# Fewer weight blocks split ahead at the end of the down products, and three of a chunk's additions to x by ScalarE and a transfer

## The chip, the core and the metric

The kernel runs on one core of a Trainium2 chip. The metric is the device time of one execution in microseconds (us). The engines are TensorE (PE; its weight loads are PEld), VectorE (DVE), ScalarE (ACT), GpSimd (POOL) and SyncE (SP); all run beside each other and wait for each other by semaphores. Transfers are issued by SP, ACT or POOL and are carried out by 16 DMA engines.

## What is computed

A decoder trunk of two layers on x of 1024 tokens by 1024 channels in float32. Each layer adds a mixer, a cross attention on a memory of 256 tokens and a feed-forward part (hidden width 2816) to x, each on a normalised x:

```python
def rmsnorm(x, g):
    xf = x.astype(jnp.float32)
    y = xf * lax.rsqrt(jnp.mean(xf * xf, axis=-1, keepdims=True) + EPS)
    return (y * g.astype(jnp.float32)).astype(x.dtype)

def swiglu(h, w_gate_up, w_down):
    g, u = jnp.split(h @ w_gate_up, 2, axis=-1)
    return (jax.nn.silu(g) * u) @ w_down

def reference(...):
    for layer in range(DEPTH):
        h = rmsnorm(x, norm_mix_g[layer])
        ...
        x = x + mix
        mem_n = rmsnorm(mem, mem_norm_g[layer])
        x = x + memory_cross_attention(rmsnorm(x, norm_xattn_g[layer]), mem_n, ...)
        x = x + swiglu(rmsnorm(x, norm_ffn_g[layer]), ffn_w_gate_up[layer], ffn_w_down[layer])
    return rmsnorm(x, final_norm_g)
```

## The kernel before

x stands transposed in SBUF: 16 tiles of 128 channels by 512 tokens, `xT[h][k]` (h is the half of the tokens, k the block of channels). Each float32 product is made of three float32r matmuls (`mm3`): each operand is split into a high part (a cast by ScalarE, L344 for weights, tile whi) and a low part (a subtraction by VectorE, L345, tile wlo). There are four buffers for each part of a weight block.

Large products use a scheme of seven block products in place of eight: sums of weight blocks (s1 to s4) meet sums of operands (t1 to t4). The weight sums are made by transfers that accumulate in SBUF, which POOL issues (`add_to`, L339). Each sum has a due time, and `pair_blocks` gives the blocks of one pair out in a fixed order.

The feed-forward part (`ffn`) runs over 22 blocks of the hidden width. For each, `gate_up` makes gate and up products in seven weight blocks of 12 matmuls; their evacuations by ScalarE (L2038) and VectorE lead to a tile of hidden values. Two such tiles make a chunk: after the third, fifth and each further odd number of blocks, `down.out(c)` multiplies chunk c with its part of the down weights (class `Down`). `Down.FORM` lists the seven weight blocks of a chunk, the operand, the group of four PSUM banks (a, b or c) that it goes into, and the part of x. For each of a block's four pieces m, `out` issues three matmuls and one VectorE instruction that adds the bank to x or subtracts it (L204); a bank that is used again is accumulated further. There are eight PSUM banks in all. Ten chunks go this way in each of the two layers; the last two blocks go through `outproj` (`down_last`). The operands of a later chunk are built beside this by `build`, spread by `pace`, which only the feed-forward's `Down` has.

What is issued when is set by a planner that runs while the program is written: `Threads` holds generators by rank, and a clock `now` that each matmul moves on by 0.42 ns per column. `prefetch` splits weight blocks until `ahead` of them are ready (3 in most of `ffn`), but a sum only when by that clock it has landed, unless `block` needs it at once. `Step` holds a transfer back until it is due. The order in which the text issues instructions gives their rank; the program places one that is ready before one that is not.

`norm_stats` sums squares over the channels with matmuls (ssq), works out the inverse root (ncol) and, `D2` of planned time later, broadcasts it with matmuls (rbp) for the evacuations. `late_stats` calls it with a delay that comes from D1 or D3. The first mixer, both cross attentions and the second mixer use it; the feed-forward's norm (`norm_quarter`) doesn't.

Of the kernel before, what the change touches and what calls it, by code (L numbers as in the profile page):

```python
# [9 lines left out]
F32 = mybir.dt.float32  # L10
# [8 lines left out]
P = 128  # L19
# [3 lines left out]
HT = 512  # L23
# [9 lines left out]
class Event:  # L33
    def __init__(self):
        self.at = None
# [80 lines left out]
class Down:  # L116
# [10 lines left out]
    def __init__(self, t, tags, eng=None, sign=1, pace=None):  # L127

        self.t, self.tags, self.eng, self.sign, self.pace = t, list(tags), eng or t.nc.vector, sign, pace
        t.th.free[self] = len(self.tags)  # L130
        self.over = {-1: Event()}
        t.th.set(self.over[-1])
        self.full, self.right, self.ev = {}, {}, {}

# [18 lines left out]
    def build(self, c):  # L153
# [8 lines left out]
        def operand(nm, src, fresh=True):  # L162
            if self.pace and fresh:
                yield self.pace / 2
            yield (self, 2)
            self.right[c, nm] = self.parts(src, self.eng)
            t.th.set(self.ev[c][nm], 2500)
            if self.pace:
                yield self.pace / 2 if fresh else self.pace
# [16 lines left out]
        t.nc.vector.scalar_tensor_tensor(b11, b11, -1.0, b21, op0=ALU.mult, op1=ALU.subtract)  # L186
        yield from operand("t4", b11)

    def out(self, c):
        t, nc, banks = self.t, self.t.nc, {}  # L190
        for w, r, to, i, h, sign in self.FORM:
            hi, lo = t.block()
            t.prefetch()
            yield self.ev[c][r]
            op = "tensor_add" if sign * self.sign > 0 else "tensor_sub"
            rh, rl, mine = self.right.pop((c, r))
            for m in range(4):
                new = (to, m) not in banks
                if new:
                    banks[to, m] = t.ps("dn")  # L200
                ps = banks[to, m]
                t.mm3(ps, [(hi[:, m, :], lo[:, m, :])], [(rh, rl)], first=new, onto=not new)
                x = t.xT[h][4 * i + m]
                getattr(nc.vector, op)(x, x, ps)  # L204
                t.prefetch()
                if m % 2:
                    yield 0
            self.give(mine)
        t.th.set(self.over[c])


# [10 lines left out]
class Trunk:  # L222
# [4 lines left out]

    D1, D2, D3 = 15000, 6000, 20000  # L230
    PARTS = ((0, slice(0, HT)), (1, slice(0, 256)), (1, slice(256, HT)))
    BUFS = {"xg": 32, "g": 20, "o": 8, "p": 7, "pt": 4, "r": 4, "rb": 2}
    RAWS = 5
# [30 lines left out]
    def mm(self, out, lhsT, rhs, start=True, stop=True, onto=False):  # L264
        n = rhs.free_size() if hasattr(rhs, "free_size") else int(np.prod(rhs.shape[1:]))
        self.th.now += max(n * (0.42 if rhs.dtype != F32 else 1.69), 55.0)
        self.nc.tensor.matmul(out, lhsT, rhs, start=start, stop=stop, skip_group_check=onto)  # L267

    def tr(self, out, src, k=P):
        self.th.now += 109.0  # L270
        self.nc.tensor.transpose(out, src, self.ident[:k, :k])  # L271
# [228 lines left out]
    def late_stats(self, N, h, rows):  # L500

        nc, acc = self.nc, None
        yield 3000
        for t in self.xT[h]:
            sq = self.g("p" if acc else "pt", name="sq")
            nc.scalar.activation(sq, t, AF.Square)
            if acc is None:
                acc = sq
            else:
                nc.vector.tensor_add(acc, acc, sq)  # L510
            yield 800
        yield from self.norm_stats(N, h, acc, rows, (self.D1 if rows else self.D3) - 9400)

    def norm_half(self, N, h, gname, off=0, rows=True):

# [1498 lines left out]
    def ffn(self, N, layer, on_half, on_block=None):  # L2014
        nc, th = self.nc, self.th
        last = FB // 2 - 1
        hid, hid_ev = [[None, None], [None, None]], [Event(), Event()]
        down = Down(self, ["pt"] * 4 + ["g"] * 4 + ["r"] * self.BUFS["r"], nc.vector, -1, 2400)
# [83 lines left out]
        def gate_up_plain():  # L2102

            ws = [[], []]

            def evac(h, gp, up):
                yield N.rb_ev[h]
                t = self.g("p", name="f")
                nc.vector.tensor_mul(t, gp, N.rb[h])
                yield 1500  # L2110
                nc.scalar.activation(t, t, AF.Silu)
                yield 1200
                nc.vector.scalar_tensor_tensor(t, t, -1.0, up, op0=ALU.mult, op1=ALU.mult)
                nc.vector.tensor_mul(t, t, N.rb[h])
                yield from hidden(0, h, t)

            for h, first, second in ((0, "11", "21"), (1, "12", "22")):
                ps = [self.ps("gu"), self.ps("gu")]
                for i, b in enumerate((first, second)):
                    yield N.b_ev[b]  # L2120
                    for n in range(2):
                        if h == 0:
                            ws[i].append(self.block())
                        self.mm3(ps[n], self.ks(ws[i][n]), N.b[b], i == 0, i == 1)
                        if h == 0 and i == 0:
                            self.prefetch()
                        yield 0
                    if b == "12":
                        th.set(N.free12, 0)
                        self.prefetch()  # L2130
                th.spawn(evac(h, *ps))

        def down_last():
            return self.outproj(hid, hid_ev, on_half, on_block=on_block, sub=True)

        for j in range(FB):
            self.ahead = 3 if 0 < j < FB - 1 else 2
            yield from gate_up(j) if j else gate_up_plain()
            if j == 1:
                yield N.rb_ev  # L2140
            if j % 2 == 0 and j:
                yield from down.out(j // 2 - 1)
        yield from down_last()


# [109 lines left out]
```

## Time and profile before

| | us |
|---|---|
| median of three timed runs | 2538.11 |
| lowest and highest of them | 2534.14, 2538.69 |
| the profiled execution | 2531.58 |
| its span, first to last instruction | 2529.9 |
| TensorE busy in the span | 2473.7 |
| VectorE busy | 1955.1 |
| ScalarE busy | 1082.3 |
| GpSimd busy | 450.9 |

An engine's busy time is the union of its instructions' times. Matmuls are pipelined, so that one starts before the last has ended: a stretch in which TensorE is always busy can still be longer than its matmuls need. In the views below, "a <- b" after an idle time says which instruction ended the wait. Names such as wraw<-wraw are what an instruction writes and reads.

### The profile page before, as it was taken

What the parts mean: (1) busy time and instruction counts of PE and PEld (TensorE: products, weight loads), DVE (VectorE), ACT (ScalarE), POOL (GpSimd) and SP (SyncE); (2) the same over time, 40 slices, a digit from 0 to 9 for tenths busy, and PEclk for the clock granted to TensorE, in tenths of its full rate; (3) what the DMA queues carried; (4) which work ended last, traced back from release to release, by engine and by line L of the source; (5) the groups of instructions that cost most, each with busy time, mean ns of one, the idle gap of its engine ahead of it and who ended that gap; (6) DMA issues with size and microseconds to landing.
All of it is one profiled execution on the core that took longest, in us unless ns stands there. A gap on an engine that the chain in (4) does not pass through costs nothing.

```text
span 2529.9 us, 34429 instructions
## 1 busy us (share of the span) xinstructions
PE 2473.7 (98%) x12029; PEld 2027.8 (80%) x12029; DVE 1955.1 (77%) x3789; ACT 1082.3 (43%) x2125; POOL 450.9 (18%) x487
## 2 busy tenths in 40 slices
PE   9999999999999999999999999999999999999998
PEld 7788888777777777779998788788777777777777
DVE  5777779988888887774638788787998777888887
ACT  5322555533333333343324367575554333333333
POOL 5411021121222122110000120001111212121222
PEclk9999999999999999999999999999999999999999
DMA  5232212455555555511122132122135555555552
GB/s 139 54 83 81 92 47 58 87 120 121 118 122 117 115 125 122 116 42 39 39 50 55 31 81 72 46 84 51 45 80 122 118 115 117 117 122 120 119 119 97
DMA packets 300093, 227.33 MB, mean 90 GB/s; under 512 B 28911, under 2 KB 250320, under 8 KB 299920
## 3 DMA queue, kind: packets, MB, share of 16 engines
q1 hardware_dynamic: 226688, 150.28, 20.5%
q0 software_dynamic: 72912, 74.32, 18.9%
q8 instruction: 95, 1.56, 0.3%
q14 instruction: 78, 0.64, 0.1%
q10 hardware_dynamic: 320, 0.53, 0.1%
HBM read 176.84 MB, written 4.19 MB: 72 GB/s over the span
## 4 chain that ended last, share of the span: by engine, by line
PE 75%; DVE 13%; DMA 4%; issue 4%; ACT 3%; POOL 1%; SPq 0%; DVEq 0%; ACTq 0%; POOLq 0%
PE gu L267 25%; PE pj L267 14%; PE dn L267 12%; PE op L267 6%; DVE x L204 4%; PE tp L267 4%; DMA wraw<-wraw 3%; DVE wlo L345 3%; PE as L267 2%; PE ao L267 1%; DMA wraw<-in_ffn_w_down_dram 1%; DVE fh L139 1%; PE apt L271 1%; PE o L267 1%; PE kps L267 1%
## 5 line engine op out<-in xcount | busy, mean ns | idle before, releaser
L344 ACT CAST whi<-wraw 128x512 fp32r<-128x512 f32 (+1 forms) x652 | 398.8, 617 | 929.4 <-DMA wraw<-wraw 207.7
L345 DVE TENSOR_TENSOR wlo<-wraw,whi 128x512 fp32r<-128x512 f32 (+1 forms) x652 | 442.2, 686 | 176.4 <-ACT whi L344 170.4
L267 PE MATMUL dn<-fh,whi 128*128 128x512 f32 x1456 | 459.9, 397 | 14.7 <-DVE x L204 11.0
L204 DVE TENSOR_TENSOR x<-x,dn 128x512 f32<-128x512 f32 x728 | 451.5, 677 | 0.3 <-PE dn L267 0.2
L267 PEld LDWEIGHTS dn<-fh,whi 128*128 128x128 f32 x1456 | 266.1, 188 | 100.8 <-issue 22.8
L267 PE MATMUL dn<-fh,wlo 128*128 128x512 f32 x728 | 286.0, 393 | 0.0
L267 PE MATMUL gu<-xth,whi 128*128 128x512 f32 x672 | 267.2, 398 | 8.9 <-DVE f L2063 3.1
L267 PE MATMUL gu<-xtl,whi 128*128 128x512 f32 x672 | 264.9, 394 | 0.7 <-DVE xtl L286 0.7
L267 PE MATMUL gu<-xth,wlo 128*128 128x512 f32 x672 | 265.0, 394 | 0.0
L267 PE MATMUL pj<-xgh,whi 128*128 128x512 f32 x592 | 238.7, 403 | 2.1 <-DVE x L204 2.1
L267 PE MATMUL pj<-xgl,whi 128*128 128x512 f32 x592 | 231.3, 391 | 0.0
L267 PE MATMUL pj<-xgh,wlo 128*128 128x512 f32 x592 | 231.3, 392 | 0.0
L267 PE MATMUL gu<-xgh,whi 128*128 128x512 f32 x568 | 224.1, 394 | 0.2
L267 PE MATMUL gu<-xgh,wlo 128*128 128x512 f32 x568 | 222.0, 391 | 0.0
L267 PE MATMUL gu<-xgl,whi 128*128 128x512 f32 x568 | 221.7, 390 | 0.0
L339 POOL DMA_DIRECT2D wraw<-in_ffn_w_gate_up_dram x84 | 116.1, 1382 | 509.1 <-DVE x L204 119.6
L339 POOL DMA_DIRECT2D wraw<-wraw x136 | 124.9, 918 | 390.0 <-DVE wlo L345 141.4
L267 PEld LDWEIGHTS dn<-fh,wlo 128*128 128x128 f32 x728 | 136.7, 188 | 31.2
L267 PEld LDWEIGHTS gu<-xth,whi 128*128 128x128 f32 x672 | 126.7, 189 | 42.8 <-ACT f L2038 8.3
L267 PEld LDWEIGHTS gu<-xtl,whi 128*128 128x128 f32 x672 | 126.9, 189 | 29.2 <-DVE xtl L286 1.6
L267 PEld LDWEIGHTS gu<-xth,wlo 128*128 128x128 f32 x672 | 126.9, 189 | 29.1
L267 PEld LDWEIGHTS pj<-xgh,whi 128*128 128x128 f32 x592 | 111.7, 189 | 25.8 <-issue 2.7
(494 smaller groups left out, 4736.5 us busy)
## 6 DMA issues: line engine op xcount, KB each, us to landing
wraw<-in_ffn_w_gate_up_dram SPq DMA_DIRECT2D x218, 256.0 KB, 3.0
wraw<-wraw POOLq DMA_DIRECT2D x136, 256.0 KB, 3.4
wraw<-in_ffn_w_down_dram SPq DMA_DIRECT2D x108, 256.0 KB, 2.8
wraw<-in_ffn_w_gate_up_dram POOLq DMA_DIRECT2D x84, 256.0 KB, 5.1
wraw<-in_od_w_in_dram SPq DMA_DIRECT2D x42, 256.0 KB, 2.8
wraw<-in_ffn_w_down_dram POOLq DMA_DIRECT2D x40, 256.0 KB, 4.5
wraw<-in_ev_w_in_dram SPq DMA_DIRECT2D x32, 256.0 KB, 2.6
wraw<-in_xattn_wkv_dram SPq DMA_DIRECT2D x32, 256.0 KB, 2.7
```

What stands on the lines that cost most here:

```text
L139: eng.tensor_sub(lo, src, hi.bitcast(F32))
L204: getattr(nc.vector, op)(x, x, ps)
L267: self.nc.tensor.matmul(out, lhsT, rhs, start=start, stop=stop, skip_group_check=onto)
L271: self.nc.tensor.transpose(out, src, self.ident[:k, :k])
L339: return Step(self.th, lambda: self.nc.gpsimd.dma_start(out=raw, in_=src, accum_op=ALU.add), delay, before)
L344: self.nc.scalar.copy(hi, raw)
L345: (eng or self.nc.vector).tensor_sub(lo, raw, hi.bitcast(F32))
```

## The change

- `Down` remembers its last transfer (`self.last`); `drain` issues it at once if it is still held back.
- In `out`, where `pace` is set, `t.ahead` is set per block of a chunk to min(ahead, 6 - n), but at least 1 (n counts from 0): 3, 3, 3, 3, 2, 1, 1. It is put back at the end of the chunk.
- For the blocks "12", "s3" and "22", the fourth piece (m is 3) is no longer added by VectorE. ScalarE copies the bank (negated by `mul`, where it is to be subtracted) into a tile of one buffer ("cring"), and a transfer issued by POOL adds that tile to x, due 1200 after.
- `ffn` calls `drain` before `down_last`.
- `D2` goes from 6000 to 8500, and the delay that `late_stats` gives where `rows` is set grows by 2500.

```diff
-        self.over = {-1: Event()}
+        self.over, self.last = {-1: Event()}, None
...
+    BY_DMA = ("12", "s3", "22")
+
+    def drain(self):
+        if self.last is not None:
+            self.last.flush()
+            self.last = None
+
     def out(self, c):
         t, nc, banks = self.t, self.t.nc, {}
-        for w, r, to, i, h, sign in self.FORM:
+        ahead = t.ahead
+        for n, (w, r, to, i, h, sign) in enumerate(self.FORM):
+            if self.pace:
+                t.ahead = max(1, min(ahead, 6 - n))
             hi, lo = t.block()
...
-                getattr(nc.vector, op)(x, x, ps)
+                if self.pace and m == 3 and w in self.BY_DMA:
+                    self.drain()
+                    tmp = t.cp.tile([P, HT], F32, tag="cring", name="dt")
+                    if op == "tensor_add":
+                        nc.scalar.copy(tmp, ps)
+                    else:
+                        nc.scalar.mul(tmp, ps, -1.0)
+                    self.last = t.add_to(x, tmp, 1200)
+                else:
+                    getattr(nc.vector, op)(x, x, ps)
...
+        t.ahead = ahead
         t.th.set(self.over[c])
...
-    D1, D2, D3 = 15000, 6000, 20000
+    D1, D2, D3 = 15000, 8500, 20000
...
-        yield from self.norm_stats(N, h, acc, rows, (self.D1 if rows else self.D3) - 9400)
+        yield from self.norm_stats(N, h, acc, rows, (self.D1 + 2500 if rows else self.D3) - 9400)
...
+        down.drain()
         yield from down_last()
```

## Rows read from the trace of the kernel before

**Rows 1.** The page: engines' busy time, share, instructions; then the chain that ended last.

```profile
PE 2473.7 (98%) x12029; PEld 2027.8 (80%) x12029; DVE 1955.1 (77%) x3789; ACT 1082.3 (43%) x2125; POOL 450.9 (18%) x487
...
PE 75%; DVE 13%; DMA 4%; issue 4%; ACT 3%; POOL 1%; SPq 0%; DVEq 0%; ACTq 0%; POOLq 0%
```

**Rows 2.** Stretches of gate and up products: start:end, length, engines' busy time, clock, DMA.

```profile
819.52:858.10 38.58, 38.58 (x168) 31.61 (x169) 27.60 (x45) 16.31 (x29) 7.90 (x8) 1.00 0.58 123
...
sum 701.62, PE 698.54 PEld 568.02 DVE 498.84 ACT 292.07 POOL 146.89; mean PE 38.81 PEld 31.56 DVE 27.71 ACT 16.23 POOL 8.16
```

**Rows 3.** The same view of the 20 stretches of down products in both feed-forward parts.

```profile
680.40:700.73 20.33, 20.25 (x86) 15.39 (x84) 19.63 (x34) 5.30 (x9) 3.86 (x4) 1.00 0.58 116
740.24:760.25 20.01, 20.01 (x86) 15.38 (x84) 19.31 (x33) 5.30 (x10) 3.48 (x3) 1.00 0.59 118
799.30:819.52 20.22, 20.17 (x86) 15.38 (x84) 19.52 (x34) 5.39 (x9) 3.75 (x4) 1.00 0.58 117
...
978.46:998.49 20.03, 20.03 (x85) 15.37 (x84) 19.33 (x33) 5.42 (x10) 3.48 (x3) 1.00 0.59 118
1037.11:1059.47 22.36, 20.43 (x85) 15.31 (x84) 21.66 (x37) 6.42 (x11) 4.08 (x4) 1.00 0.54 106
...
sum 420.49, PE 406.79 PEld 306.41 DVE 402.91 ACT 112.90 POOL 82.45; mean PE 20.34 PEld 15.32 DVE 20.15 ACT 5.65 POOL 4.12
```

**Rows 4.** VectorE in order of time in the stretch of 680.40: start, us, what, count.

```profile
690.32 0.68 DVE L345 TENSOR_TENSOR wlo<-wraw,whi 128x512 fp32r<-128x512 f32 x1
690.92 2.47 DVE L204 TENSOR_TENSOR x<-x,dn 128x512 f32<-128x512 f32 x4
693.31 0.68 DVE L345 TENSOR_TENSOR wlo<-wraw,whi 128x512 fp32r<-128x512 f32 x1
```

**Rows 5.** TensorE in order of time in the same stretch.

```profile
691.27 0.39 PE L267 MATMUL dn<-fh,wlo 128*128 128x512 f32 x1
691.74 0.70 PE L267 MATMUL dn<-fh,whi 128*128 128x512 f32 x2
692.28 0.39 PE L267 MATMUL dn<-fh,wlo 128*128 128x512 f32 x1
692.51 0.62 PE L267 MATMUL dn<-fh,whi 128*128 128x512 f32 x2
```

**Rows 6.** Tile x: who waited for its instructions (us, times).

```profile
  PE dn L267: 11.0, 21
```

**Rows 7.** Groups by line and form: count, busy us, mean ns, idle before.

```profile
L2038 ACT COPY f<-gu 128x512 f32<-128x512 f32 x128 | 74.3, 580 | 1.3 <-DVE f L2070 0.7 <-PE gu L267 0.5
...
L339 POOL DMA_DIRECT2D wraw<-wraw x136 | 124.9, 918 | 390.0 <-DVE wlo L345 141.4 <-DMA wraw<-wraw 120.7 <-DVE x L204 61.3
```

**Rows 8.** The page: the software queue; one kind of transfer, median us to landing.

```profile
q0 software_dynamic: 72912, 74.32, 18.9%
...
wraw<-wraw POOLq DMA_DIRECT2D x136, 256.0 KB, 3.4
```

**Rows 9.** TensorE in order of time at the second mixer's start; idle before in brackets.

```profile
1124.29 0.95 PE L267 MATMUL ssq<-ones,sq 128*128 128x1 f32 x8
1128.80 1.02 PE L271 MATMUL rbp<-ident,ncol 128*128 128x128 f32 x4 [3.57 <-DVE ncol L530]
```

**Rows 10.** Waits: who waited for whom, us in total, times, longest.

```profile
DVE wlo L345 <- ACT whi L344: 170.4, 125, 10.2
```

**Rows 11.** ScalarE in order of time at the start of gate products after 700.73.

```profile
703.54 0.62 ACT L344 CAST whi<-wraw 128x512 fp32r<-128x512 f32 x1 [1.65 <-PE gu L267]
704.06 0.58 ACT L2038 COPY f<-gu 128x512 f32<-128x512 f32 x1
```

## The prediction

> **What bounds the kernel now.** I read the page first: TensorE is busy for 98% of the span and carries 75% of the chain that ended last, VectorE 13% [rows 1]. So a change on other engines can only give back time in which TensorE stands still, and its busy figure does not show that, because overlapping matmuls count as busy. I therefore cut the two feed-forward layers into stretches and compared lengths. All 18 full stretches of gate and up products (168 matmuls, two pairs) take 701.62 us; the undisturbed one shown takes 38.58, which is 0.2297 us a matmul or 2.756 a block of 12 [rows 2]. At that step a stretch of down products (84 matmuls, seven blocks) would take 19.29 us. The 20 stretches take 420.49 [rows 3], so 34.7 us are lost in them: 0.7 to 3.1 each. That is the most that can be won there.
>
> Who takes it? In these stretches VectorE is busy 402.91 of 420.49 us [rows 3]. Its own order of time shows why: per block one low half (wlo) and four additions to x follow each other without a gap, and from one wlo to the next pass 2.99 us [rows 4]. Four additions in 2.47 us with the last one lasting 0.68 means a new one every 0.60; five slots are 3.0 us. TensorE needs 2.756 for the same block. Its timeline shows the difference as a pause at each block's edge: starts are 0.23 us apart, but from 691.27 to 691.74 pass 0.47 [rows 5]. The wait is for the PSUM banks: block k+2 writes or adds into banks that the additions of block k must have read (PE dn waited for x 21 times, 11.0 us, in the long waits alone [rows 6]). So block k+2 cannot start before the first addition of block k is done, and once VectorE is a whole block behind, TensorE runs at VectorE's pace.
>
> **The change, part by part.** *Three additions move.* In the second, fifth and seventh block of a chunk ("12", "s3", "22") the fourth addition leaves VectorE: 60 in all, three slots or 1.8 us a stretch. *Fewer splits ahead.* `ahead` falls from 3 to 2 in the fifth block and 1 in the last two. The next pair's "11" and "12", which were split in the fifth and sixth block, come in the last one and behind the stretch; their two wlo slots leave the blocks where they stand before additions.
>
> What that gives follows from the slots between first additions, counted in blocks 1 to 7. From the second's to the third's there are five slots, after the change four: block five may start 0.60 earlier. From the third's to the fourth's, five as before. From the fourth's to the fifth's, five, after it four (no wlo): 2.4 us, below TensorE's 2.756, so block six's surplus of 0.23 goes; from the fifth's to the sixth's three, so block seven's goes too. In sum 0.60 + 0.23 + 0.23 = 1.06 us a stretch, where the stretch lost that much. Four lost less: 680.40, 740.24, 799.30 and 978.46 lose 1.04, 0.72, 0.93 and 0.74 [rows 3], of which I let 0.07 stand each: 3.1 in all. The other 16 give 17.0. **Gain 20.1 us**; 14.6 of the 34.7 stay, above all what is lost before the fifth block, as in the stretch of 1037.11, which lost 3.1.
>
> *What takes their place.* 60 ScalarE copies from PSUM, 0.580 us each by the nearest row [rows 7]: 1.7 us a chunk on an engine that is busy 112.90 of 420.49 us [rows 3]; they free their bank sooner than VectorE, which is a block behind. Hidden; but a copy stands in ScalarE's queue behind casts that wait for a weight, so the price is 0 to, where one is held, the rest of a block (2.7 us); what a bank that is free sooner could gain is in the last case below. I take 0, as casts wait mostly at a block's edge. 60 accumulating transfers, issued by POOL at 0.918 us each [rows 7] with 3.4 us from issue to landing by the same size and kind [rows 8]. POOL is busy 82.45 of 420.49 us there [rows 3], so 2.8 us a chunk fit beside it. Nobody reads that x until the next chunk, some 55 us later (after the last chunk, some 25 us), so landing costs nothing. The one buffer ("cring") is free again after 0.58 + 0.92 + 3.4 = 4.9 us and is wanted after two blocks at the earliest, 5.5. POOL waits for the copy with the weights' own accumulations queued behind it; that is a rival below.
>
> *Due times.* D2 rises by 2500 and the late sums of squares by 2500 where `rows` holds. Four places see it: the first mixer, both cross attentions, the second mixer. Each moves a broadcast, sums or an attention behind other matmuls that exist anyway. At the second mixer TensorE now stands 3.57 us waiting for the column factors, with all earlier projections done [rows 9]; nothing is put in there by the change. Taking 0, the bounds are -3.6 (that wait is filled) and +10 (four places at 2.5 each, exposed).
>
> **Sum.** The profiled execution took 2531.58 us, span 2529.9. It lies 6.5 us below the median of the three timed runs, 2538.11, and below the lowest, 2534.14. So 2531.6 - 20.1 = 2511.5 on its own scale; the same difference from the median gives **2518**.
>
> **Rivals.** *The weights' transfers take the wait over.* VectorE's low halves wait for casts, and these for transfers: 125 waits, 170.4 us [rows 10], and such a wait stands in front of additions. The software queue's 74.32 MB now take 18.9% of 16 engines' span [rows 8], that is 1.7 us of all engines for 256 KB; 60 more are 15.7 MB, 101 us. If in each chunk one x transfer (0.9 us of POOL, 1.7 us of the engines) lies ahead of an accumulation that VectorE waits for, some 1 us a chunk is lost again: 20 us, no change, 2538. Against it: the waited-for transfers precede a stretch, and the x transfers are issued in its third and sixth block and just behind it. The Trainium skill (DMA: Bandwidth & Descriptors, Issuing engines are not separate DMA queues) says that transfers of all issuing engines interleave on the same 16 DMA engines, which speaks for this rival; by that rule alone the gain would go and 2538 come out. The stretches' DMA share of 0.54 to 0.59 [rows 3] shows room, but not whether it lies at the right moment.
>
> *The splits come too late* (the other side). With one block in hand, "11" is split at the last block, and its sum "s2" is added 3500 of planned time later and held landed 4500 after that, so "s2" is split only when the third gate block asks for it, in the text behind the addition of "12" and the gate's product. If VectorE keeps that order, the addition starts when block "12" ends (5.28 + 0.39 us [rows 5]), then 0.60 + 0.60 + 0.68: low half at 7.55, wanted by the block's third matmul at 5.51 + 0.46 = 5.97. 1.6 us lost in each of 20 chunks is 32; less 20 it is 12 slower: 2550. It decides from the point where a split written later is not placed earlier. Against it: at 703.54 ScalarE runs a cast ahead of the copy at 704.06 [rows 11], though the copy (L2038, end of a block) is written first and the cast belongs to the next block's `prefetch`. So the program's order is not the text's; what is ready goes first, and s2's transfer should land some 2.5 us into the gate products.
>
> *The change frees more than counted*: the freed slots also catch up on blocks three and four, say 27 us: 2511.
>
> **How the numbers follow.** Forecast 0.62 (2512 to 2526), more than counted 0.08, taken over by transfers 0.15 (2531 to 2541), too late 0.15 (2543 to 2557). A difference under 0.2% (5 us) is about what a measurement of this kernel cannot tell from none. Faster: the first two and a little of the third, 0.71; same 0.14; slower 0.15. The range reaches from 2508 to 2541 and leaves out the late splits and the extreme of the rest; the norm places' bounds (-3.6, +10) around the forecast lie inside it.
>
> **What would show it.** Right: the 20 stretches sum to about 400 us, their last three blocks at 2.76; x additions by VectorE 668 instead of 728; gate stretches still 38.6 to 39.8. Wrong, by transfers: POOL's wraw transfers land later, VectorE's wait for whi rises over 170 us, stretches stay near 21. Wrong, by late splits: a pause of 1 to 2 us in front of or within the third gate block, gate stretches at 40 or more. A shift of the four norm places by over 2 us would make the sum wrong in either direction.

## The result and the profile after

| | before | after |
|---|---|---|
| median, us | 2537.38 | 2622.14 |
| lowest to highest | 2532.79 to 2538.69 | 2619.77 to 2626.69 |
| profiled execution | 2531.58 | 2619.77 |
| its span | 2529.9 | 2618.0 |

The changed kernel takes 1.034 times as long, with a 95% interval of 1.0327 to 1.0354: 3.4% slower, where 0.8% faster was forecast and the range ended at 2541.

The page of the changed kernel, first its engines and then the software queue and the transfer that is new (packets, MB, share; KB each, median us to landing), says nothing of this by itself:

```profile
PE 2505.2 (96%) x12029; PEld 2042.3 (78%) x12029; DVE 1923.9 (73%) x3729; ACT 1108.9 (42%) x2186; POOL 502.9 (19%) x547
...
q0 software_dynamic: 81552, 90.05, 22.0%
...
x<-dt POOLq DMA_DIRECT2D x60, 256.0 KB, 4.3
```

VectorE has its 60 additions less, POOL its 60 transfers more. The stretches tell where the time went. The 20 stretches of down products (start:end, length, each engine's busy time, granted clock, DMA share, GB/s), to be laid beside [rows 3]:

```profile
701.77:721.87 20.10, 19.91 (x86) 15.62 (x84) 19.09 (x32) 6.55 (x12) 5.26 (x5) 1.00 0.66 129
...
1025.26:1044.58 19.32, 19.32 (x85) 15.78 (x84) 19.17 (x32) 5.87 (x11) 4.40 (x4) 1.00 0.66 130
...
sum 408.79, PE 397.45 PEld 311.78 DVE 385.14 ACT 133.16 POOL 101.62; mean PE 19.87 PEld 15.59 DVE 19.26 ACT 6.66 POOL 5.08
```

They gained: 408.79 us where 420.49 stood, 11.7 less. The 18 full stretches of gate and up products in the same view, beside [rows 2]:

```profile
721.87:766.43 44.56, 41.23 (x170) 32.14 (x168) 27.18 (x45) 16.68 (x30) 9.79 (x11) 0.96 0.59 120
...
851.02:892.19 41.17, 39.69 (x170) 31.16 (x168) 26.30 (x43) 16.03 (x29) 9.59 (x10) 1.00 0.61 123
...
sum 787.35, PE 732.29 PEld 572.65 DVE 488.34 ACT 296.64 POOL 176.43; mean PE 40.68 PEld 31.81 DVE 27.13 ACT 16.48 POOL 9.80
```

They lost 85.7 us (787.35 against 701.62), 4.8 each, though no line of their code changed. With 8.1 us lost in the first and last gate stretches of each layer and 6.3 in the first mixer, less the 11.7, this accounts for the 88.1 us by which the span grew, to within 0.3.

One such stretch, from 721.87, shows how. POOL first, in order of time (start, us, what, idle before it and what ended it):

```profile
718.49 0.88 POOL L359 DMA_DIRECT2D x<-dt  x1 [0.26 <-issue]
723.74 0.86 POOL L359 DMA_DIRECT2D x<-dt  x1 [4.37 <-ACT dt L218]
724.32 1.18 POOL L359 DMA_DIRECT2D wraw<-wraw  x1
```

ScalarE and TensorE at the same place:

```profile
722.78 0.59 ACT L218 COPY dt<-dn 128x512 f32<-128x512 f32 x1 [5.61 <-DMA x<-dt]
...
730.12 1.14 ACT L364 CAST whi<-wraw 128x512 fp32r<-128x512 f32 x2 [4.11 <-DMA wraw<-wraw]
...
730.79 0.50 PE L287 MATMUL gu<-xth,whi 128*128 128x512 f32 x1 [3.06 <-ACT whi L364]
```

And the landing of that one wraw<-wraw transfer (KB, us from issue to landing):

```profile
wraw<-wraw POOLq DMA_DIRECT2D x1, 256.0 KB, 5.7
```

Read from the bottom up: TensorE stands 3.06 us in front of the third gate block, for a cast; the cast waited for the sum s2, which landed at 730.0; that transfer took 5.7 us and was issued only at 724.32, 2.45 us into the gate products; in front of it in POOL's queue stands the transfer of the last piece of x ("22"), which waited for ScalarE's copy, which waited for the one buffer, from which the piece of "s3" had not yet landed. In the kernel before the same sum was issued 3.4 us ahead of the gate products, which began at 700.73:

```profile
694.75 1.31 POOL L339 DMA_DIRECT2D wraw<-in_ffn_w_gate_up_dram  x1 [6.53 <-DVE x L204]
697.29 0.90 POOL L339 DMA_DIRECT2D wraw<-wraw  x1 [1.24 <-DVE wlo L345]
```

So the x transfer makes the sum late in two ways: it stands in front of it, and it has not landed yet when the sum is issued, 0.58 us behind it. The 5.7 us of this stretch are the worse case: in four of the 18 stretches the sum took 5.3 to 6.0 us, in the other 14 it took 4.2 to 4.3, and before it took 3.3 to 3.5.

The waits of the changed kernel (who for whom, us, times, longest) say that such waits recur: TensorE's in front of the third gate block stands in all 18 stretches. The first two are new, and of the last two the list of before has none:

```profile
POOL x L359 <- ACT dt L218: 84.7, 19, 4.9
ACT dt L218 <- DMA x<-dt: 82.7, 16, 6.2
PEld gu L287 <- ACT whi L364: 48.7, 20, 3.6
PE gu L287 <- ACT whi L364: 40.2, 20, 3.2
```

The pause has a second price. The stretch around it (as above; before the comma the length, near the end the granted clock):

```profile
727.29:730.80 3.51, 0.45 (x3) 0.03 (x2) 0.03 (x1) 0.68 (x2) 0.15 (x1) 1.00 0.25 43
730.80:734.30 3.50, 3.50 (x9) 2.49 (x10) 3.50 (x6) 1.50 (x3) 0.71 (x1) 0.56 0.67 125
```

After it nine matmuls start in 3.50 us where fifteen would: the granted clock is 0.56 of full speed on the mean, nearly all of it at the lower level (1.2 GHz). 11 of the 18 stretches show a clock of 0.96; 0.04 of 44 us is 1.75 us each, some 19 of the 85.7.

### The profile page after: what moved, and what is told of

Read it like the earlier page. It is cut to its first block, busy times and chain, and to the rows that moved or that the text cites. A ratio compares the mean times of both kernels' runs of the same rounds, so it can differ in the third digit from the quotient of the medians.

```text
span 2618.0 us, 34460 instructions
## 1 busy us (share of the span) xinstructions
PE 2505.2 (96%) x12029; PEld 2042.3 (78%) x12029; DVE 1923.9 (73%) x3729; ACT 1108.9 (42%) x2186; POOL 502.9 (19%) x547
## 3 DMA queue, kind: packets, MB, share of 16 engines
q1 hardware_dynamic: 226688, 150.28, 20.2%
q8 instruction: 94, 1.54, 0.2%
## 5 line engine op out<-in xcount | busy, mean ns | idle before, releaser
L365 DVE TENSOR_TENSOR wlo<-wraw,whi 128x512 fp32r<-128x512 f32 (+1 forms) x652 | 445.9, 689 | 294.3 <-ACT whi L364 291.2
L223 DVE TENSOR_TENSOR x<-x,dn 128x512 f32<-128x512 f32 x668 | 415.0, 680 | 0.4 <-PE dn L287 0.4
L287 PE MATMUL gu<-xth,whi 128*128 128x512 f32 x672 | 278.5, 414 | 64.7 <-ACT whi L364 40.2
L287 PE MATMUL gu<-xth,wlo 128*128 128x512 f32 x672 | 275.3, 410 | 0.0
L287 PE MATMUL gu<-xtl,whi 128*128 128x512 f32 x672 | 273.5, 407 | 0.7 <-DVE xtl L306 0.7
L359 POOL DMA_DIRECT2D wraw<-in_ffn_w_gate_up_dram x84 | 109.7, 1305 | 482.9 <-DVE x L223 133.7
```

What stands on the lines that cost most here:

```text
L359: return Step(self.th, lambda: self.nc.gpsimd.dma_start(out=raw, in_=src, accum_op=ALU.add), delay, before)
L365: (eng or self.nc.vector).tensor_sub(lo, raw, hi.bitcast(F32))
```

## The experiments

All are of the whole program. The table holds what the runs and traces gave, as means over the 18 gate stretches: when s2 of a stretch's first pair was issued and landed, counted from the stretch's first matmul; the length of blocks two and three together (undisturbed 5.5); the landing of the second pair's s2, counted from the start of the ninth block (that pair's second); the length of the ninth block (undisturbed 2.76); and the sums of the down and gate stretches.

| kernel | ratio to before, 95% | median | s2 issued, landed | blocks 2+3 | second s2 | ninth | down | gate |
|---|---|---|---|---|---|---|---|---|
| before | 1 | 2537.4 | -3.4, -0.1 | 5.44 | -3.26 | 2.90 | 420.5 | 701.6 |
| after | 1.0327 to 1.0354 | 2622.1 | 2.6, 7.2 | 8.83 | -2.15 | 3.75 | 408.8 | 787.4 |
| e1_ahead_only | 1.0159 to 1.0195 | 2583.4 | 1.6, 5.1 | 6.15 | -1.54 | 4.28 | 418.6 | 754.0 |
| e2_additions_only | 1.0014 to 1.0034 | 2543.1 | -3.1, 2.1 | 5.45 | -1.99 | 3.85 | 417.6 | 718.7 |
| e3_due_only | 1.0007 to 1.0026 | 2542.5 | -3.4, -0.1 | 5.44 | -3.22 | 2.93 | 424.1 | 702.8 |
| e4_no_due | 1.0319 to 1.0353 | 2621.5 | 2.6, 7.2 | 9.00 | -1.78 | 4.20 | 408.7 | 798.7 |
| e5_sum_at_once | 1.0302 to 1.0337 | 2617.5 | 2.7, 7.2 | 9.11 | -2.27 | 3.68 | 405.7 | 791.6 |
| e7_no_transfers | 1.0138 to 1.0171 | 2576.2 | 0.9, 4.3 | 5.56 | -1.22 | 4.66 | 406.1 | 747.7 |
| e8_ahead_two | 1.0088 to 1.0118 | 2563.7 | -1.3, 2.3 | 5.44 | -1.30 | 4.54 | 408.9 | 736.8 |
| e9_last_by_vector | 1.0124 to 1.0159 | 2571.1 | 1.1, 4.4 | 6.08 | -1.49 | 4.34 | 409.0 | 745.9 |
| e10_extra_before_sum | 1.0085 to 1.0113 | 2561.5 | -3.5, -0.1 | 5.44 | -1.65 | 4.20 | 422.3 | 730.2 |
| e11_d2_only | 1.0005 to 1.0023 | 2540.6 | -3.4, -0.1 | 5.44 | -3.21 | 2.89 | 424.2 | 702.8 |
| e12_first_only | 0.9975 to 0.9994 | 2533.2 | -3.2, 0.9 | 5.47 | -2.47 | 3.46 | 410.4 | 713.1 |

### The parts alone

Theory A puts the loss on late sums through the lowered ahead, theory B on the x transfers in POOL's queue.

**The lowered ahead alone**, in the kernel before:

```diff
...
+            if self.pace:
+                t.ahead = max(1, min(ahead, 6 - n))
...
```

> The kernel before with the lowered ahead alone (3, 3, 3, 3, 2, 1, 1); all additions by VectorE, old due times. Theory A (late sums: with fewer splits in hand, block 11 of the next pair is split at the end of the down products, so its sum s2 is transferred late and TensorE stands in front of the third gate block): this edit alone lengthens each of the 18 gate stretches from 38.6-39.8 to 41-45 us, and the time is 2590 to 2625. Theory B (the x transfers hold the sums: POOL waits for a ScalarE copy into the one buffer, which waits for the transfer before, with the weights' sum queued behind): nothing of that is here, gate stretches stay at 38.6-39.8, the down stretches gain 0.2 to 0.5 us each, and the time is 2527 to 2538.

**The additions alone**, ahead at 3 and the old due times; the diff is the change's own without the two lines above and without D2 and late_stats.

> The three additions by ScalarE copies and transfers alone; ahead stays 3, old due times. Theory A (late sums through the lowered ahead): the sum s2 is issued some 3 us before the gate products as in the kernel before, gate stretches stay at 38.6-39.8, the 20 down stretches lose 0.6 to 1 us each, and the time is 2518 to 2530. Theory B (x transfers hold the weights' sums): POOL still waits for the copy and the copy for the one buffer, so gate stretches are 41-45 and the time is 2590 to 2625.

**The due times alone:**

```diff
-    D1, D2, D3 = 15000, 6000, 20000
+    D1, D2, D3 = 15000, 8500, 20000
...
-(self.D1 if rows else self.D3) - 9400
+(self.D1 + 2500 if rows else self.D3) - 9400
```

> The later due times alone (D2 8500 and the late sums of squares 2500 later). Theories A and B: only the first mixer's projections change, from 10.5 to 94.3 us before to 10.5 to 100.6 us, as in the changed kernel, so 2541 to 2546. Theory C (the 6 us of the first mixer come from somewhere else than the due times, the placing of the program's instructions having shifted): 2535 to 2540.

**Both parts without the due times**, the change with the second diff undone:

> The changed kernel without the later due times: lowered ahead and the three additions by transfers. Theories A and B: the loss of the feed-forward parts stays whole, only the first mixer's 6 us go: 2614 to 2619. Theory C (the due times have no part in it): 2620 to 2625. That the two edits hurt only together (the late sum meets the x transfer in POOL's queue) would show as both single edits under 2550 and this one over 2610.

The lowered ahead alone costs 46 us, the additions 5, the due times 5. Both parts together cost 84, so 33 us belong to neither alone. Neither theory holds whole. A is right that the lowered ahead costs by itself (2583, just under its 2590), but the additions alone win nothing (2543, above its 2530). B names what happens in the changed kernel, but with ahead at 3 it doesn't: there s2 stands in front of the last x transfer in POOL's queue, lands at 2.1, and the time is far from B's 2590. The due times come out as expected (2542.5 in 2541 to 2546), yet undoing them in the changed kernel gives nothing that can be measured (2621.5, where theories A and B said 2614 to 2619 and theory C, which the run of the due times alone contradicts, 2620 to 2625): its first mixer is 6.7 us shorter (93.88 against 100.58), its gate stretches 11.3 longer in the profiled execution, and why these differ stays open.

What the lowered ahead does alone is seen on VectorE at the end of a chunk, in the gate stretch from 583.34:

```profile
578.70 5.46 DVE L207 TENSOR_TENSOR x<-x,dn 128x512 f32<-128x512 f32 x9
584.08 0.68 DVE L349 TENSOR_TENSOR wlo<-wraw,whi 128x512 fp32r<-128x512 f32 x1
584.68 2.47 DVE L207 TENSOR_TENSOR x<-x,dn 128x512 f32<-128x512 f32 x4
587.07 0.68 DVE L349 TENSOR_TENSOR wlo<-wraw,whi 128x512 fp32r<-128x512 f32 x1
```

and on TensorE:

```profile
584.82 0.50 PE L271 MATMUL gu<-xgh,wlo 128*128 128x512 f32 x1 [0.41 <-DVE wlo L349]
587.81 0.50 PE L271 MATMUL gu<-xgh,wlo 128*128 128x512 f32 x1 [0.43 <-DVE wlo L349]
```

Nine additions without a gap stand in front of the low half of "11", four more in front of that of "12"; TensorE waits for both. This is late by VectorE's backlog, and the first half of what the rival of the late splits said. s2 itself lands at 5.1, in time: in no stretch does TensorE wait in front of the third block. The larger loss of this kernel is further on: its ninth block takes 4.28 us.

### POOL's queue

Two theories were put for the interaction. P: the planner's due time holds s2 back. Q: POOL's queue does, in which x's last transfer stands in front.

**s2 due at once**, in the changed kernel:

```diff
-            step[nm] = step[place] = self.add_to(raw[place], src, 3500 if before else 1000, before)
+            step[nm] = step[place] = self.add_to(raw[place], src, 0 if nm == "s2" else 3500 if before else 1000, before)
```

> The changed kernel with the sum s2 due at once behind the split of block 11 instead of 3500 of planned time later. Theory P (the planner's due time makes the sum late): s2's transfer is issued some 3 us earlier than the 2.57 us behind the start of the gate products at which it stands in the changed kernel, the stall of 2.1 to 3.4 us there goes, time 2560 to 2595. Theory Q (POOL's queue makes it late: the transfer of the stretch's last piece to x stands in front of s2 and waits for ScalarE's copy of the last bank, so s2 cannot start before some 2.5 us into the gate products whatever it is due): s2 still issued at 2 to 3 and landed at about 7, time 2610 to 2630.

P falls: the sum is issued at 2.7 and lands at 7.2, as before the edit, and the time is 2617.

**The copies without the transfers**, in the changed kernel:

```diff
-                    self.last = t.add_to(x, tmp, 1200)
```

> The changed kernel with the 60 copies by ScalarE but without the 60 transfers (those pieces are never added to x: that part of the sum is left out). It prices the transfers with all else unchanged. Theory Q (POOL's queue and the transfers' landing): s2 is issued at 0 to 1.7 us behind the gate products' start and landed by 5.1, the stall in front of the third gate block goes, gate stretches 39.5 to 42, time 2545 to 2580. Theory A (the late split itself, through VectorE and ScalarE, holds the third block): gate stretches stay at 43 or more, time 2600 to 2620.

**The last block's piece by VectorE again:**

```diff
-    BY_DMA = ("12", "s3", "22")
+    BY_DMA = ("12", "s3")
```

> The changed kernel with the last block's fourth piece (22) added by VectorE again, 12 and s3 by copy and transfer. Nothing of x stands in front of s2 behind the stretch. Theory Q: s2 is issued at 0 to 2 us and lands at 4 to 5.5, gate stretches 40 to 42, time 2555 to 2590, near the kernel with the lowered ahead alone (2583) or below it. Theory T (each transfer costs its share): two thirds of the interaction of 33 us stay, 2598 to 2612.

**Ahead not below 2**, all three transfers kept:

```diff
-                t.ahead = max(1, min(ahead, 6 - n))
+                t.ahead = max(2, min(ahead, 6 - n))
```

> The changed kernel with ahead never below 2 in a chunk (3, 3, 3, 3, 2, 2, 2). Block 11 is split a block earlier, and in POOL's program s2 then stands in front of the transfer of the last piece to x, not behind it. Theory Q: s2 lands at 1 to 4 us, the stall in front of the third gate block goes, gate stretches 39.5 to 41, time 2540 to 2562. Theory T (the transfers as such cost, by the engines and queue they share, wherever they stand): the interaction of some 33 us stays, 2580 to 2600.

Each takes x's last transfer from in front of s2, in its own way, and in each the stall in front of the third block goes: blocks two and three take 5.56, 6.08 and 5.44 us instead of 8.83 (in the second, TensorE still waits 0.4 us for the low half of "12"). The second is the clearest: ahead is as in the changed kernel, 40 of the 60 transfers are still there, and one piece moved back to VectorE takes 51 us off. In the third all 60 transfers are there and their order differs, but block 11 is also split a block earlier, so it does not test the order alone. Its POOL in order of time, where the gate products begin at 585.61:

```profile
582.24 0.88 POOL L359 DMA_DIRECT2D x<-dt  x1
584.46 0.86 POOL L359 DMA_DIRECT2D wraw<-wraw  x1 [1.34 <-DVE wlo L365]
587.94 0.86 POOL L359 DMA_DIRECT2D x<-dt  x1 [2.62 <-DMA wraw<-wraw]
588.90 0.86 POOL L359 DMA_DIRECT2D wraw<-wraw  x1
```

The sum goes first, 1.15 us ahead of the gate products, and the piece of x behind it. ScalarE's copies wait for their one buffer here as long as in the changed kernel (83.9 us in 16 waits, against 82.7 in 16), but here nothing stalls the third block: not the wait by itself, but what is queued behind it, was the price. A second buffer for the copies was not tried. Theory T, that each transfer costs its share wherever it stands, falls by the second run: 2571 where it said 2598 to 2612.

The order is not all of it. Against the kernel without transfers, s2 in the changed kernel is issued 1.6 us later on the mean (2.57 against 0.93) and then takes 1.25 us longer to land (4.58 against 3.33). I read the first part as the place in the queue and the second as the transfer beside it.

Q's gate stretches came out in all three (41.5, 41.4 and 40.9 us on the mean), and its times but for the last, 1.7 us above its 2562. Of what is left over before, 27 to 39 us, most is the ninth block: 26 to 32 us over the 18 stretches.

### The ninth block

In every kernel with the lowered ahead or the additions TensorE waits once more, in front of the second pair's third block, and there the profile names another cause: ScalarE's copy of a bank (f<-gu, L2038 before), which must free the bank of "11" before s2's products are added in it. In the kernel before, ScalarE and TensorE in order of time:

```profile
599.99 0.62 ACT L344 CAST whi<-wraw 128x512 fp32r<-128x512 f32 x1 [4.50 <-DMA wraw<-wraw]
...
605.69 0.58 ACT L2038 COPY f<-gu 128x512 f32<-128x512 f32 x1
...
606.32 0.50 PE L267 MATMUL gu<-xth,whi 128*128 128x512 f32 x1 [0.29 <-ACT f L2038]
```

From the cast of s2, which waits for the landing, to the copy pass 5.70 us: gate multiplications, the Silu and two casts of hidden values that ScalarE and VectorE hand to each other in a fixed order. It is just in time: TensorE waits 0.29. Theory R says that a later landing is passed on whole; theory O that another order of instructions makes the stall. **An extra transfer in front of the second pair's s2**, in the kernel before:

```diff
...
+            if nm == "s2" and getattr(order, "mark", False):
+                emit = lambda e=emit: (self.nc.gpsimd.dma_start(out=self.dummy, in_=src, accum_op=ALU.add), e())
...
```

> The kernel before with one more thing: in front of the sum s2 of each second gate pair of a stretch (18 of them) a further transfer of 256 KB adds the same source into a tile that nobody reads. Ahead, additions and due times as before. Theory R (the hand-over behind the sum is just in time: 5.7 us of VectorE and ScalarE work in fixed order lie between the landing of the second pair's s2 and the copy that frees the bank for that pair's third block, so a later landing is passed on whole): the sum lands 1.5 to 2.5 us later, the ninth block of a gate stretch grows from 2.90 to 3.8 to 4.6 us, the first pair's blocks hardly change, time 2553 to 2580. Theory O (the stall of the second pair in the changed kernels comes from another order of instructions on ScalarE and not from the landing): block nine stays under 3.2, time 2536 to 2543.

POOL, ScalarE and TensorE of this kernel at the same place:

```profile
598.11 0.88 POOL L401 DMA_DIRECT2D dummy<-wraw  x1 [4.73 <-DMA wraw<-in_ffn_w_gate_up_dram]
598.67 1.21 POOL L343 DMA_DIRECT2D wraw<-wraw  x1
...
603.33 0.62 ACT L348 CAST whi<-wraw 128x512 fp32r<-128x512 f32 x1 [5.88 <-DMA wraw<-wraw]
...
609.03 0.58 ACT L2048 COPY f<-gu 128x512 f32<-128x512 f32 x1
...
609.66 0.50 PE L271 MATMUL gu<-xth,whi 128*128 128x512 f32 x1 [1.68 <-ACT f L2048]
```

Again 5.70 us from cast to copy, and the wait is 1.68. One transfer of 256 KB per stretch, with ahead, additions and due times as before, costs 1.0% (25 us), and blocks two and three do not change. R holds against O, though the landing is not passed on whole: it is 1.6 us later on the mean, and the ninth block 1.3 us longer. The sum is issued only 0.5 us later there; the other 1.1 us are its slower landing beside the extra transfer. The column of the second s2 in the table shows the same in all thirteen kernels: the later it lands against the ninth block's start, the longer the block, from -3.26 with 2.90 through -2.47 with 3.46, -1.99 with 3.85 and -1.65 with 4.20 to -1.22 with 4.66, with no exception larger than 0.04. (Part of this is argued from the order of the table, not from one edit each.)

Why does the second sum come late when only the first pair's was moved? By the kernel's text, loads wait for a free buffer, and a buffer is free when its block has been split; no run tried the buffers, so this path is argued. In the means of the traces the first pair's s2 lands 5.2 us later with the lowered ahead, 2.2 with the additions and 7.3 with all; the second pair's is issued at 15.4 us of the stretch before and at 18.4, 16.4 and 20.2 in these three, 3.0, 1.0 and 4.8 later. By then the stretch itself has lost 1.2, 0 and 3.6 us, so that against the ninth block's start the sum is issued 1.8, 1.0 and 1.1 us later. A part of the lateness comes back.

### The due times, and a smaller form

**D2 alone:**

```diff
-    D1, D2, D3 = 15000, 6000, 20000
+    D1, D2, D3 = 15000, 8500, 20000
```

> The kernel before with D2 at 8500 alone; the sums of squares keep their old due time. If the broadcast of the column factors, moved later, makes the first mixer's projections longer, they take 98 to 100 us here too and the time is 2540 to 2545. If the later sums of squares make it, they take 94 to 95 and the time is 2534 to 2539.

The first mixer's projections take 98.85 us where they took 94.32, as with both due times (98.97): D2 makes it. The end of that part before, in the view of the stretches, and TensorE's wait in it:

```profile
85.00:104.55 19.55, 18.60 (x80) 14.76 (x79) 9.61 (x15) 4.23 (x8) 7.12 (x8) 1.00 0.34 70
```

```profile
87.27 1.10 PE L267 MATMUL pps<-pd,poolw 128*128 128x512 f32 x2 [0.95 <-DVE pd L805]
```

The same with D2 alone:

```profile
84.30:108.35 24.05, 20.09 (x80) 15.64 (x79) 12.98 (x19) 7.96 (x13) 7.57 (x10) 0.93 0.23 47
```

```profile
89.43 1.53 PE L267 MATMUL pps<-pd,poolw 128*128 128x512 f32 x2 [3.96 <-DVE pd L805]
```

The broadcast comes later, the chain of the mixer's pooling behind it too, and TensorE's wait for it grows from 0.95 to 3.96 us; the stretch's granted clock is 0.93 on the mean where it was 1.00.

**A smaller form**, the additions of "12" only, with ahead 3, 3, 3, 3, 3, 2, 2 and the old due times:

```diff
-    BY_DMA = ("12", "s3", "22")
+    BY_DMA = ("12",)
...
+                t.ahead = max(2, min(ahead, 7 - n))
```

> A smaller form of the change: only block 12's fourth piece by copy and transfer, ahead 3, 3, 3, 3, 3, 2, 2, old due times. In POOL's program nothing of x stands near the sums s2, and block 11 of the next pair is split in the fifth block as before. Theories Q and R: s2 is issued 3 to 3.5 us ahead of the gate products as in the kernel before, gate stretches stay at 38.6 to 39.8, the down stretches lose 0.3 to 0.5 us each, time 2526 to 2537. Theory T (any further transfer or later split costs): gate stretches 39.8 or more on the mean, time 2539 to 2552.

It is 0.15% faster than before (0.06 to 0.25), less than what counts as a difference here. It shows the exchange in small: 10.1 us won in the down stretches of the profiled execution, 11.5 lost in the gate stretches, most of it in the ninth block (3.46 against 2.90), with s2 landing at 0.9 instead of -0.1. Theories Q and R expected the time and the means of the stretches but not this lateness, since no x transfer stands near the sum. In the trace block 12, now split a block later, has its own sum s4 issued at 2.2 us instead of 0.5, and s2 takes 4.1 us to land instead of 3.3; which of the two holds the ninth block wasn't told apart. No form tried is clearly faster than the kernel before.

## Why the prediction was wrong

**What bounds the down products: right, with little over half the size.** VectorE's slots did set their pace, and the stretches gained 11.7 us where 20.1 were forecast. By blocks one to seven the means went from 2.74, 2.77, 3.08, 3.39, 3.05, 2.99, 2.99 to 2.75, 2.86, 2.82, 3.38, 3.03, 2.86, 2.74. The 0.46 of blocks six and seven became 0.38. The 0.60 of block five did not come: its start went from 11.99 to 11.80 us of the stretch. From the second block's first addition to the third's pass 3.00 us where 3.60 passed (six slots before, not the five that I counted, since the low part of an operand, fh, stands there too; the difference is the one slot forecast). But VectorE reaches the first addition of all later (3.37 instead of 3.07 us into the stretch), so that the third block's first addition is 0.30 earlier instead of 0.60 (10.86 against 11.16); the kernel without the transfers has 3.11, so that they have a part in it, but how is open, as is why block four still took 3.38. Nor does one part alone win this: the additions alone gave 2.9 us, the lowered ahead 1.9, both 11.8.

**The steps that failed: fewer splits ahead and the x transfers, both at nothing in the sum.** The sum counts what the lowered ahead gives in the down products and no price for it in the gate products; the price stood only in a rival. By itself it costs 46 us. The x transfers were taken at 0: they cost 5 us alone and 33 more together with the lowered ahead. I asked when x is read again (far off: right) and when the buffer is free (after 4.9 us, wanted after 5.5: 16 copies waited). I named that POOL waits with the weights' accumulations queued behind it, but left it to a rival at 1 us a chunk. Of the changed kernel's loss some 50 us hang on the one transfer that stands in front of s2 (ratios 1.034 and 1.014 with that piece by VectorE).

**The transfers' rival came true, alone.** With the additions alone the gate stretches lose 0.95 us each, by the ninth block, and the time is 2543 where this rival said 2538. In the traces s2 takes longer beside an x transfer that was issued 0.6 us ahead of it: a median of 5.3 us with the additions alone and 4.3 in the changed kernel, against 3.3 before. The rule of the Trainium skill that I weighed there (DMA: Bandwidth & Descriptors, Issuing engines are not separate DMA queues) is about transfers of different issuing engines; here POOL issues both, so no run here tests it. The DMA share of a whole stretch, 0.54 to 0.59 [rows 3], was no argument against it: what decides lies in some 6 us around the stretch's end.

**The late splits' rival came true, larger.** It put a loss of 32 us on 20 chunks; the gate stretches lost 52 with the lowered ahead alone. Its place was partly right: low halves come late behind VectorE's backlog, but those of "11" and "12", not that of s2. My argument against it, that what is ready goes first, fails where an engine has no gap: in that trace VectorE did nine additions before the low half of "11". And "lands some 2.5 us into the gate products" was 5.1 alone, since s2 is issued only behind that low half (at 1.6), and 7.2 in the change, where the x transfer stands in front of it as well.

**What no case held: the second pair.** I treated a late sum as one loss at the third block. The second pair's sum is late too, and there stood a hand-over of 5.7 us with TensorE already waiting 0.3 behind it. This cost 1.4 us a stretch with the lowered ahead and 0.85 in the change. A wait of 0.29 in the trace of before was the sign: the landing of that sum had next to no slack.

**Due times: in the bounds, not at the value.** I took 0 of -3.6 to +10; the runs gave 4.7 for both (1.8 to 6.6) and D2 makes it. The second mixer, at which I looked, hardly changed (229.1 after against 228.6 before); the first did.

**The signs named were the right ones.** A pause in front of the third gate block, gate stretches over 40, and VectorE's wait for whi, 291.2 us where [rows 10] have 170.4: they stood for the two rivals, and both were there, with 33 us more than their sum. The signs of a right forecast came as far as the down products went: 668 additions, blocks six and seven at 2.86 and 2.74, a sum of 409 instead of 400.

## What to carry to other kernels

When a transfer is added to a queue that carries the operands of the next stage, write out that queue's order for the moment of the hand-over: what the new transfer waits for, what stands behind it, and what moves beside it count more than its own landing or its free buffer. When work done ahead is cut to relieve one engine, follow the supply chain for its whole period, through the buffers it frees, and look for waits near zero in front of the bound engine: they show where no slack is left. Two edits that each lose a little can meet in one queue and lose more than their sum.

## What was not expected of the hardware

An accumulating transfer of 256 KB from SBUF to SBUF (s2) landed after 3.3 to 3.5 us in the kernel before. With another issued some 0.6 us ahead of it, it landed after 4.2 to 4.3 us in 14 stretches of the changed kernel and after 5.3 to 6.0 in the other four, and after a median of 5.3 with the additions alone. What makes some of them slower than others stays open. A due time moved in the planner's clock did nothing to the order of POOL's queue (s2 issued at 2.7 us with 0 as with 3500, which gave 2.6). And the length of a pause alone doesn't tell whether the clock falls: in the kernel with the lowered ahead, the stretch from 583.34 has a pause of 3.0 us at 609.27 and kept its clock, that from 647.14 has one of 2.6 and did not:

```profile
583.34:626.47 43.13, 39.41 (x170) 31.30 (x168) 28.16 (x46) 15.99 (x29) 8.74 (x9) 1.00 0.56 116
647.14:691.33 44.19, 40.81 (x170) 32.38 (x168) 29.45 (x48) 16.38 (x29) 9.61 (x10) 0.96 0.56 114
```
